# The last projection of a streaming-encoder layer: seven products for eight over pairs of chunks

## The chip, the cores and the metric

The kernel runs on one core of a Trainium2 chip. The metric is device time in microseconds (us) of one execution, lower is better. A core has five engines with a queue of instructions each: TensorE (in the profile PE, with its weight loads as PEld), VectorE (DVE), ScalarE (ACT), GpSimd (POOL) and SyncE (SP), which here issues the DMA transfers. They work side by side and wait for each other through semaphores. SBUF is the working memory with 128 partitions, PSUM takes what TensorE accumulates, and HBM is the large memory outside.

## The reference

One layer on a sequence of 2048 rows with 1024 channels, in float32. Two branches (a causal convolution and stick-breaking attention) are gated and merged to `y`, and a last projection goes back to the residual stream:

```python
mod = c_act @ w_ada[l] + b_ada[l]
shift, scale, gate = jnp.split(mod[:, None, :], 3, axis=-1)
h = rms_norm(x, norm_g[l]) * (1.0 + scale) + shift
u = h @ w_in[l]
...
y_a = conformer_conv_branch(glu_in, gate_a, w_dw[l], b_dw[l], ln_g[l], ln_b[l], w_conv_out[l])
...
o = stick_breaking_attention(q, k, v).reshape(bsz, seq, D_SB)
y_b = (o * jax.nn.silu(gate_b)) @ w_sb_out[l]
y = jax.nn.sigmoid(m_a) * y_a + jax.nn.sigmoid(m_b) * y_b
x = x + gate * (y @ w_out[l])
```

The last line is what is changed: a matrix of 1024 x 1024 times `y`, for 2048 columns.

## The kernel before

Everything lies with channels on the partitions. The 1024 channels are eight rows of 128 (`KC`), the 2048 positions are four chunks of 512 (`CH`, `NCH`). A float32 product is made of three float32r matmuls (`mm3`, line 135): each operand is split into a rounded part, cast by ACT, and a rest, subtracted by DVE (or POOL, for weights in `load_piece`); then hi x hi, hi x lo and lo x hi are added in PSUM.

The kernel has three parts: projections and convolution; attention, with the filling of merge gates between its steps; and the last stage, which this change is about. Its pieces:

- `y_tiles(ch, ...)` (line 1035) makes the gated sum of a chunk. For each of eight rows it multiplies the outputs of the two branches (`za`, `zb`, four tiles each) by the combined weights `w_cs`, 2 x 4 x 3 matmuls into PSUM tiles `p`; DVE multiplies them by the merge gates `ma` and `mb` loaded from HBM, adds them, and the sum is split into `yh` (ACT, line 1061) and `yl` (DVE, line 1062).
- `load_za` and `load_zb` (lines 1012, 1022) load the branch outputs of a chunk through small buffers `io` (four of them, shared with the gates and the tiles of x) and split them by `split_z` (line 1008); for `zb`, POOL first multiplies attention output and gate (line 1030).
- `out_tile(ch, j, ...)` (line 1067) is the last projection for one row of one chunk: 8 x 3 matmuls into a PSUM tile `po`, then one DVE operation (line 1073) that multiplies by `gate` and adds x, and a store.
- The weights `w_out` stay in SBUF: `resident` (line 999) loads and splits them once, during the first chunk; row 0 in pool `wr`, on the left side of SBUF, rows 1 to 7 in pool `wor` on the right. The `w_cs` rows 2 to 7 are in `wr` too. The tiles of `y` and `z` are in pool `yp` on the left.

Chunk 0's gated sums begin while attention ends (from `others`, line 1115): from there on the memory of the normalised input is free, and pools `wr` and `yp` take it. The order afterwards (line 1166): rest of chunk 0's gated sums, loads of chunk 1's `z` tiles, eight `out_tile`s of chunk 0, gated sums of chunk 1, and so on. TensorE's order is written out by hand only through attention (`pin`); in the last stage a scheduler orders each engine's instructions ahead of time, by the order of the code and by what is ready in its own reckoning, and on the chip each engine keeps that order. All transfers of the last stage are issued on the SP queue.

Of the kernel before, what the change touches and what calls it, by code (L numbers as in the profile page):

```python
# [18 lines left out]
P = 128  # L19
# [31 lines left out]
def trunk_kernel(  # L51
# [122 lines left out]
    def hT(g):  # L174
        return hT_[g]

# [695 lines left out]
    with ExitStack() as s2:  # L872
# [124 lines left out]
        wcs, wo = {}, {}  # L997
# [7 lines left out]
        def io(name):  # L1005
            return yp.tile([P, CH], F32, tag="io", name=name, bufs=4)
# [4 lines left out]

        def load_za(ch):
            z = []
            for kc in range(JC):
                t = yp.tile([P, 2, CH], F32R, tag=f"za{kc}", name=f"za{kc}")
# [6 lines left out]
        def load_zb(ch):  # L1022
            z = []
            for kc in range(JC):
                t = yp.tile([P, 2, CH], F32R, tag=f"zb{kc}", name=f"zb{kc}")
# [9 lines left out]
        def y_tiles(ch, za, zb, psum, y):  # L1035

            for j in range(KC):
# [20 lines left out]
                nc.vector.tensor_tensor(out=ma, in0=ma, in1=mb, op=ALU.add)  # L1058
                hi = yp.tile([P, CH], F32R, tag=f"yh{j}", name=f"yh{j}")
                lo = yp.tile([P, CH], F32R, tag=f"yl{j}", name=f"yl{j}")  # L1060
                nc.scalar.copy(out=hi, in_=ma)
                nc.vector.tensor_tensor(out=lo, in0=ma, in1=f(hi), op=ALU.subtract)
                y[0].append(hi)
                y[1].append(lo)
                yield

        def out_tile(ch, j, y, psum):
            ts_ = slice(ch * CH, (ch + 1) * CH)
            xt = io("xt")
            nc.sync.dma_start(xt, x_t[j][:, ts_])  # L1070
            ps = psum("po")
            dense(ps, wo[j], y, KC)
            nc.vector.scalar_tensor_tensor(out=xt, in0=ps, scalar=gate[:, j:j + 1], in1=xt,
                                           op0=ALU.mult, op1=ALU.add)
            nc.sync.dma_start(out_t[j][:, ts_], xt)
# [16 lines left out]
        prev = held = ygen = wr = yp = None  # L1092
        y = ([], [])
# [5 lines left out]
        for n_, u in enumerate(units + [None]):  # L1099
# [15 lines left out]
            def others(q, half):  # L1115

                nonlocal nf, ny, ygen, wr, yp
# [5 lines left out]
                if q == LAST and not half:  # L1123
# [3 lines left out]
                    with tc.high_priority(offset=0):  # L1127
                        za = load_za(0)
                        zb = load_zb(0)
                        wcs[1] = load_piece(wpa, w_cs[1])  # L1130
                    ygen = y_tiles(0, za, zb, lambda n: psum(n), y)
# [34 lines left out]
    with s3:  # L1166
        wor = s3.enter_context(tc.tile_pool(name="wor", reuse_waits="tile", bufs=1, side="right"))
        pd = s3.enter_context(tc.tile_pool(name="pd3", reuse_waits="tile", bufs=2, space=PSUM))
        psum = lambda n: pd.tile([P, CH], F32, tag=n, name=n, bufs=4 if n == "po" else 2)
        for ch in range(NCH):  # L1170
            if ch:
                y = ([], [])
                ygen = y_tiles(ch, za, zb, psum, y)
# [58 lines left out]
```

## Time and profile before

| | |
|---|---|
| median of 3 runs | 1876.35 us (1873.36 to 1876.59) |
| the profiled execution's own time | 1877.81 us |
| its span in the profile | 1876.1 us |
| granted TensorE clock, mean | 0.993 |
| first `po` matmul | at 1560.6 us |

The span is from the first to the last recorded instruction of the profiled execution. A row of grouped instructions names line, engine, operation, the tiles written and read, shapes and count; then busy time and mean duration in ns, then the engine's idle time before them and what ended it. A row in order of time has the start, the duration and what ran. The table's last row is from the view of the tile `po`.

### The profile page before, as it was taken

What the parts mean: (1) busy time and instruction counts of PE and PEld (TensorE: products, weight loads), DVE (VectorE), ACT (ScalarE), POOL (GpSimd) and SP (SyncE); (2) the same over time, 40 slices, a digit from 0 to 9 for tenths busy, and PEclk for the clock granted to TensorE, in tenths of its full rate; (3) what the DMA queues carried; (4) which work ended last, traced back from release to release, by engine and by line L of the source; (5) the groups of instructions that cost most, each with busy time, mean ns of one, the idle gap of its engine ahead of it and who ended that gap; (6) DMA issues with size and microseconds to landing.
All of it is one profiled execution on the core that took longest, in us unless ns stands there. A gap on an engine that the chain in (4) does not pass through costs nothing.

```text
span 1876.1 us, 27226 instructions
## 1 busy us (share of the span) xinstructions
PE 1797.0 (96%) x9612; PEld 1517.0 (81%) x9612; DVE 1228.2 (65%) x1696; ACT 812.8 (43%) x1880; POOL 681.3 (36%) x899
## 2 busy tenths in 40 slices
PE   6899999999999998999999999999999899999999
PEld 5888889899888977778877778777788677888887
DVE  7646578888879354467777777777777895334341
ACT  5465113232231122267766777776777752010110
POOL 0343111111121143466666666666666641010100
PEclk9999999999999999999999999999999999999999
DMA  8553402325132443432232323132322446353532
GB/s 288 169 186 105 137 29 80 90 67 148 45 104 93 157 141 118 149 128 81 79 96 68 102 63 109 61 93 70 99 65 88 131 143 215 107 163 96 164 95 79
DMA packets 117596, 211.08 MB, mean 113 GB/s; under 512 B 15442, under 2 KB 27730, under 8 KB 117460
## 3 DMA queue, kind: packets, MB, share of 16 engines
q1 hardware_dynamic: 116308, 207.24, 35.5%
q10 hardware_dynamic: 1152, 2.10, 0.3%
q8 instruction: 76, 1.25, 0.3%
q14 instruction: 60, 0.49, 0.1%
HBM read 137.98 MB, written 71.30 MB: 112 GB/s over the span
## 4 chain that ended last, share of the span: by engine, by line
PE 72%; DVE 8%; POOL 6%; issue 5%; DMA 5%; ACT 4%; SPq 1%; DVEq 0%; ACTq 0%; POOLq 0%
PE pd L115 38%; PE po L115 9%; PE p L115 8%; PE av L115 5%; PE pT L120 5%; PE z L115 5%; POOL w L952 3%; DVE sc L945 2%; POOL wlo L103 1%; ACT z L941 1%; DMA xt<-in_x_n_dram 1%; PE pt L120 1%; DVE tlo L979 1%; DMA wa<-in_w_ada_dram 1%; DMA gt<-ga 1%
## 5 line engine op out<-in xcount | busy, mean ns | idle before, releaser
L952 POOL TENSOR_TENSOR w<-w,sc 128x512 f32<-128x512 f32 (+1 forms) x320 | 361.6, 1130 | 251.8 <-DVE sc L945 179.1
L115 PE MATMUL pd<-hhi,whi 128*128 128x512 f32 x1024 | 413.4, 404 | 1.0 <-ACT vsg L858 1.0
L115 PE MATMUL pd<-hhi,wlo 128*128 128x512 f32 x1024 | 402.7, 393 | 0.0
L115 PE MATMUL pd<-hlo,whi 128*128 128x512 f32 x1024 | 402.5, 393 | 0.0
L945 DVE TENSOR_TENSOR_SCAN sc<-z,sc,w 128x512 f32<-128x512 f32 x192 | 245.0, 1280 | 90.9 <-ACT z L941 83.6
L103 POOL TENSOR_TENSOR wlo<-wl,whi 128x512 fp32r<-128x512 f32 x88 | 131.3, 1503 | 401.4 <-ACT whi L102 401.2
L115 PEld LDWEIGHTS pd<-hhi,wlo 128*128 128x128 f32 x1024 | 193.5, 189 | 42.5 <-POOL wlo L103 0.2
L940 ACT ACTIVATE w<-z 128x512 f32<-128x512 f32 (+1 forms) x320 | 172.2, 538 | 125.7 <-PE z L115 100.0
L115 PEld LDWEIGHTS pd<-hhi,whi 128*128 128x128 f32 x1024 | 195.5, 191 | 35.4 <-ACT vsg L858 1.4
L115 PEld LDWEIGHTS pd<-hlo,whi 128*128 128x128 f32 x1024 | 194.3, 190 | 34.3
L979 DVE TENSOR_TENSOR tlo<-pT,thi 128x512 fp32r<-128x512 f32 (+1 forms) x320 | 184.2, 598 | 35.8 <-ACT thi L978 32.4
L115 PE MATMUL z<-kt,q 128*128 128x512 f32 (+2 forms) x640 | 192.7, 382 | 5.0 <-DVE sc L945 3.5
L978 ACT CAST thi<-pT 128x512 fp32r<-128x512 f32 (+1 forms) x320 | 165.4, 527 | 61.3 <-PE pT L120 57.4
L120 PE MATMUL pT<-ident,w 128*128 128x128 f32 x1088 | 173.1, 275 | 9.8 <-POOL w L952 9.5
L120 PEld LDWEIGHTS pT<-ident,w 128*128 128x128 f32 x1088 | 137.5, 141 | 45.9 <-POOL w L952 14.5
L115 PE MATMUL pd<-whi,hhi 128*128 128x256 f32 x608 | 169.7, 287 | 3.6 <-ACT hhi L131 1.9
L941 ACT ACTIVATE z<-z 128x512 f32<-128x512 f32 (+1 forms) x320 | 171.7, 537 | 0.0
L115 PE MATMUL pd<-whi,hlo 128*128 128x256 f32 x608 | 167.0, 285 | 2.3 <-DVE hlo L131 1.7
L115 PE MATMUL pd<-wlo,hhi 128*128 128x256 f32 x608 | 154.0, 284 | 0.0
L949 DVE TENSOR_TENSOR_SCAN sc<-z,tri 128x512 f32<-128x512 f32 (+3 forms) x128 | 104.4, 819 | 53.9 <-ACT z L941 41.9
L115 PE MATMUL av<-tlo,vt 128*128 128x512 f32 (+1 forms) x320 | 123.2, 385 | 14.0 <-DVE tlo L979 10.9
L115 PEld LDWEIGHTS z<-kt,q 128*128 128x128 f32 x640 | 109.6, 189 | 24.1 <-DVE sc L945 5.4
(284 smaller groups left out, 3108.4 us busy)
## 6 DMA issues: line engine op xcount, KB each, us to landing
wl<-in_w_in_dram SPq DMA_DIRECT2D x64, 256.0 KB, 2.9
wa<-in_w_ada_dram SPq DMA_DIRECT2D x24, 512.0 KB, 5.1
wl<-in_w_qkv_dram SPq DMA_DIRECT2D x36, 256.0 KB, 2.7
xt<-in_x_n_dram SPq DMA_DIRECT2D x16, 512.0 KB, 5.5
vst<-st SPq DMA_DIRECT2D x64, 128.0 KB, 2.0
kt<-kst SPq DMA_DIRECT2D x32, 256.0 KB, 2.8
vt<-vst SPq DMA_DIRECT2D x32, 256.0 KB, 2.7
q<-qst SPq DMA_DIRECT2D x32, 256.0 KB, 2.8
```

The costliest lines, as they stand in the source:

```text
L103: (lo_eng or nc.gpsimd).tensor_tensor(out=lo[:, s], in0=wl, in1=f(hi[:, s]), op=ALU.subtract)
L115: i = nc.tensor.matmul(*a, **k)
L120: i = nc.tensor.transpose(*a)
L940: nc.scalar.activation(out=w[:, lo:], in_=z[:, lo:], func=AF.Sigmoid, scale=HD ** -0.5)
L941: nc.scalar.activation(out=z[:, lo:], in_=z[:, lo:], func=AF.Sigmoid, scale=-HD ** -0.5)
L945: nc.vector.tensor_tensor_scan(out=s[:, 1:], data0=z, data1=w, initial=s[:, 0:1], op0=ALU.mult, op1=ALU.bypass)
L949: nc.vector.tensor_tensor_scan(out=s[:, lo + 1:], data0=z[:, lo:], data1=tri[:, :CH - lo], initial=1.0, op0=ALU.mult, op1=ALU.max)
L952: nc.gpsimd.tensor_tensor(out=w[:, lo:], in0=w[:, lo:], in1=s[:, lo:CH], op=ALU.mult)
L978: nc.scalar.copy(out=thi[:, :n], in_=pT[:, :n])
L979: nc.vector.tensor_tensor(out=tlo[:, :n], in0=pT[:, :n], in1=f(thi[:, :n]), op=ALU.subtract)
```

## The change

Chunks are taken in pairs. The last projection of a pair is a product of 2 x 2 blocks: the weights are halved by input rows and by output rows (512 x 512 each), `y` by input rows and by chunk. Instead of eight products of such blocks there are seven, of sums or differences of blocks, and each product is added to one or two blocks of the result (12 additions in all). The table `SEVEN` has, for each product, the terms of the weights, the terms of `y`, and the blocks it is added to with their signs; `LASTS` says after which product a block is complete.

- `operands` loads halves of weight rows raw (512 columns, 256 KB each) through `io`, now of eight buffers; where two terms belong to an operand POOL adds or subtracts them (`combined`); then `split_z` casts on ACT and subtracts on DVE. Weights and sums of `y` are `A` and `B`, four tiles each, in two sets with the tags `z` and `o`; these tags are also those of the `za` and `zb` tiles. One set is made while the product before uses the other. All are in `yp`, but the `B` tiles of set `o`, which are in a new pool `yr` on the right.
- `product` has 4 rows x 4 x 3 matmuls into `po`, then per row one or two DVE operations that add the product, times `gate` or its negative `ngate`, to an accumulator `acc` (12 buffers in a pool `ya`, loaded with x at its first use); a complete one is stored.
- The gated sums of a pair are made one after the other and kept unsplit as float32 (`y`); the split of `y` and the resident `w_out` are gone. Chunk 1's `z` tiles are loaded right after attention, chunk 2's during the last product of the first pair, chunk 3's before chunk 2's gated sums.

```diff
+    SEVEN = {
+        2: (((1, 0, 1), (1, 1, 1)), ((0, 0, 1),), ((1, 0, 1), (1, 1, -1))),
+        4: (((1, 1, 1),), ((1, 0, 1), (0, 0, -1)), ((0, 0, 1), (1, 0, 1))),
+        1: (((0, 0, 1), (1, 1, 1)), ((0, 0, 1), (1, 1, 1)), ((0, 0, 1), (1, 1, 1))),
+        6: (((1, 0, 1), (0, 0, -1)), ((0, 0, 1), (0, 1, 1)), ((1, 1, 1),)),
+        3: (((0, 0, 1),), ((0, 1, 1), (1, 1, -1)), ((0, 1, 1), (1, 1, 1))),
+        7: (((0, 1, 1), (1, 1, -1)), ((1, 0, 1), (1, 1, 1)), ((0, 0, 1),)),
+        5: (((0, 0, 1), (0, 1, 1)), ((1, 1, 1),), ((0, 0, -1), (0, 1, 1))),
+    }
+    LASTS = {(1, 0): 4, (1, 1): 3, (0, 0): 5, (0, 1): 5}
+    H = KC // 2
...
-            return yp.tile([P, CH], F32, tag="io", name=name, bufs=4)
+            return yp.tile([P, CH], F32, tag="io", name=name, bufs=8)
...
+        def operand(q, half, i):
+            pool = yr if (q, half) == ("o", "b") else yp
+            return pool.tile([P, 2, CH], F32R, tag=f"{q}{half}{i}", name=f"{q}{half}{i}")
...
-                t = yp.tile([P, 2, CH], F32R, tag=f"za{kc}", name=f"za{kc}")
+                t = operand("zooz"[ch], "a", kc)
...
-                nc.vector.tensor_tensor(out=ma, in0=ma, in1=mb, op=ALU.add)
-                hi = yp.tile([P, CH], F32R, tag=f"yh{j}", name=f"yh{j}")
-                lo = yp.tile([P, CH], F32R, tag=f"yl{j}", name=f"yl{j}")
-                nc.scalar.copy(out=hi, in_=ma)
-                nc.vector.tensor_tensor(out=lo, in0=ma, in1=f(hi), op=ALU.subtract)
-                y[0].append(hi)
-                y[1].append(lo)
+                y[ch, j] = (yr if ch % 2 else yp).tile([P, CH], F32, tag=f"y{j}", name=f"y{j}")
+                nc.vector.tensor_tensor(out=y[ch, j], in0=ma, in1=mb, op=ALU.add)
                 yield
...
+        def combined(terms, part, to):
+            a, b = terms[0], terms[-1]
+            if a is b:
+                return part(a)
+            t = to(a)
+            nc.gpsimd.tensor_tensor(out=t, in0=part(a), in1=part(b),
+                                    op=ALU.add if b[2] > 0 else ALU.subtract)
+            return t
+        turn = [0]
+        def operands(m, ch):
+            q = "zo"[turn[0] % 2]
+            turn[0] += 1
+            A, B = [], []
+            for j in range(H):
+                A.append(operand(q, "a", j))
+                w = {}
+                for t in SEVEN[m][0]:
+                    w[t] = io("w")
+                    nc.sync.dma_start(w[t], w_out[j + H * t[0]][:, t[1] * CH:(t[1] + 1) * CH])
+                split_z(combined(SEVEN[m][0], lambda t: w[t], lambda t: w[t]), A[j])
+                B.append(operand(q, "b", j))
+                split_z(combined(SEVEN[m][1], lambda t: y[ch + t[1], j + H * t[0]],
+                                 lambda t: io("sum")), B[j])
+            return A, B
+        acc = {}
+        def product(m, ch, A, B, psum):
+            for j in range(H):
+                ps = psum("po")
+                for kc in range(H):
+                    s = slice(kc * P, (kc + 1) * P)
+                    mm3(ps, A[j][:, 0, s], A[j][:, 1, s], B[kc][:, 0, :], B[kc][:, 1, :],
+                        kc == 0, kc == H - 1)
+                for r, c_, sign in SEVEN[m][2]:
+                    row, g = j + H * r, ch + c_
+                    ts_ = slice(g * CH, (g + 1) * CH)
+                    if (row, g) not in acc:
+                        acc[row, g] = ya.tile([P, CH], F32, tag="acc", name="acc", bufs=12)
+                        nc.sync.dma_start(acc[row, g], x_t[row][:, ts_])
+                    o = acc[row, g]
+                    nc.vector.scalar_tensor_tensor(
+                        out=o, in0=ps, scalar=(gate if sign > 0 else ngate)[:, row:row + 1],
+                        in1=o, op0=ALU.mult, op1=ALU.add)
+                    if LASTS[r, c_] == m:
+                        nc.sync.dma_start(out_t[row][:, ts_], o)
...
+                    ngate = yp.tile([P, KC], F32, name="ngate")
+                    nc.vector.tensor_scalar(out=ngate, in0=gate, scalar1=-1.0, scalar2=None,
+                                            op0=ALU.mult)
...
-        wor = s3.enter_context(tc.tile_pool(name="wor", reuse_waits="tile", bufs=1, side="right"))
+        yr = s3.enter_context(tc.tile_pool(name="yr", reuse_waits="tile", bufs=1, side="right"))
...
+        za, zb = load_za(1), load_zb(1)
+        steps(ygen)
+        steps(y_tiles(1, za, zb, psum, y))
+        ya = s3.enter_context(tc.tile_pool(name="ya", reuse_waits="tile", bufs=1, side="right"))
+        for ch in (0, 2):
             if ch:
+                za3, zb3 = load_za(3), load_zb(3)
+                steps(y_tiles(2, za, zb, psum, y))
+                steps(y_tiles(3, za3, zb3, psum, y))
+            order = list(SEVEN)
+            nxt = operands(order[0], ch)
+            for i, m in enumerate(order):
+                A, B = nxt
+                if i + 1 < len(order):
+                    nxt = operands(order[i + 1], ch)
+                elif ch == 0:
+                    za, zb = load_za(2), load_zb(2)
+                product(m, ch, A, B, psum)
```

## What was predicted, with its working

> **What bounds the kernel now.** I read the page's busy times first, then the chain of work that ended last, in order of time, then groups by line.
>
> ```profile
> span 1876.1 us, 27226 instructions
> PE 1797.0 (96%) x9612; PEld 1517.0 (81%) x9612; DVE 1228.2 (65%) x1696; ACT 812.8 (43%) x1880; POOL 681.3 (36%) x899
> ```
>
> ```profile
> 1567.41 39.93 PE po L115 x170
> 1607.33 43.52 PE p L115 x192
> 1650.86 44.64 PE po L115 x192
> 1695.50 43.52 PE p L115 x192
> 1739.03 44.64 PE po L115 x192
> 1783.67 43.52 PE p L115 x192
> 1827.19 44.66 PE po L115 x192
> 1871.85 0.02 issue
> 1871.87 0.75 DVE xt L1073
> ```
>
> The second fence has start, length and what worked. From 1567.41 us to the end nothing but TensorE stands in the chain: gated sums (`p`) and last projection (`po`) take turns, and one VectorE operation and a store follow. So this stage is worth its matmuls, and a change there counts in full unless another engine takes over. The other engines have room, as two stretches of 20 us show (columns: busy us of PE, PEld, DVE, ACT, POOL, then granted clock, DMA share, GB/s):
>
> ```profile
> 1700.00:1720.00 20.00, 20.00 (x90) 16.57 (x89) 9.94 (x15) 2.48 (x4) 0.00 (x0) 1.00 0.33 93
> 1840.00:1860.00 20.00, 20.00 (x87) 16.09 (x86) 2.25 (x3) 0.00 (x0) 0.00 (x0) 1.00 0.28 90
> ```
>
> **Matmuls.** Before, `po` has 4 chunks x 8 rows x 8 x 3 = 768 matmuls; at 44.64/192 = 0.2325 us that is 178.6 us. After, 2 pairs x 7 products x 4 x 4 x 3 = 672. `p` runs at 43.52/192 = 0.2267 us. Why `po` is slower is seen by weight row:
>
> ```profile
> L115 PE MATMUL po<-yh,wo0h x32: 389/389/505, 1560.6 to 1831.8; 128*128 128x512 f32 x32
> L115 PE MATMUL po<-yh,wo2h x32: 395/396/396, 1573.6 to 1843.0; 128*128 128x512 f32 x32
> ```
>
> (ns: shortest, median, longest.) `wo0` lies in pool `wr` on the left, `wo1` to `wo7` in `wor` on the right; the moving operand is the same. The new weights `A` all lie in `yp`, on the left, so I take 0.2267: 152.3 us. Half the products read `B` from `yr` on the right, against weights on the left; no row has that pairing. Bounds are 0.2267 and 0.2325; I take the middle for those 336, +1.0. Term: 153.3 - 178.6 = **-25.3 us** (-26.3 to -22.4).
>
> **The hand-over to the stage.** TensorE waits once:
>
> ```profile
> 1566.60 0.51 PE L115 MATMUL po<-yh,wo0h 128*128 128x512 f32 x1 [1.06 <-ACT yh L1061]
> 1567.41 0.50 PE L115 MATMUL po<-yl,wo0h 128*128 128x512 f32 x1 [0.30 <-DVE yl L1062]
> ```
>
> That is 1.36 us for the last split of `y`. After, chunk 1's gated sums follow directly and need no split of `y`; late next are chunk 1's `z` tiles, whose 12 loads take the queue places of the 16 loads of `w_out`. I take **-1** (-1.4 to 0). All 32 splits of `y` go; none was waited for otherwise.
>
> **What each product adds.** Rows for the prices (count, then busy us and mean ns):
>
> ```profile
> L1073 DVE SCALAR_TENSOR_TENSOR xt<-po,gate,xt 128x512 f32<-128x512 f32 x32 | 23.7, 750 | 100.2 <-PE po L115 92.0 <-DMA xt<-in_x_t_dram 8.2
> L1010 DVE TENSOR_TENSOR za<-n,za 128x512 fp32r<-128x512 f32 x8 | 5.5, 690 | 4.2 <-ACT za L1009 4.0
> L1010 DVE TENSOR_TENSOR zb<-o,zb 128x512 fp32r<-128x512 f32 x8 | 9.0, 1124 | 14.7 <-ACT zb L1009 14.4
> L1009 ACT CAST za<-n 128x512 fp32r<-128x512 f32 x8 | 5.0, 620 | 7.4 <-PE p L115 3.9 <-DMA n<-za 3.5
> L1030 POOL TENSOR_TENSOR o<-o,gb 128x512 f32<-128x512 f32 x8 | 10.3, 1294 | 163.3 <-DMA gb<-gb 87.2 <-DMA o<-o 76.1
> ```
>
> Per pair of chunks: 7 x 8 = 56 splits (a cast at 0.62 on ACT, a subtraction at 0.69 on DVE), 12 x 4 = 48 accumulations at 0.75 on DVE, and, counting the two-term entries of the table, 40 sums at 1.29 on POOL. Alone, ACT has 34.7 us, POOL 51.6, DVE 38.6 + 36.0 = 74.6, beside TensorE's 76.7 (153.3/2). Each engine fits, DVE barely. But they don't run side by side. The `zb` split costs 1124 ns where the same operation on `za` costs 690; in order of time:
>
> ```profile
> 1747.59 1.29 POOL L1030 TENSOR_TENSOR o<-o,gb 128x512 f32<-128x512 f32 x1 [0.59 <-DMA gb<-gb]
> 1747.68 1.74 DVE L1010 TENSOR_TENSOR zb<-o,zb 128x512 fp32r<-128x512 f32 x1 [3.01 <-ACT zb L1009]
> 1665.85 1.30 POOL L1030 TENSOR_TENSOR o<-o,gb 128x512 f32<-128x512 f32 x1 [0.35 <-DMA gb<-gb]
> 1666.19 1.51 DVE L1010 TENSOR_TENSOR zb<-o,zb 128x512 fp32r<-128x512 f32 x1 [4.05 <-ACT zb L1009]
> 1489.36 1.73 POOL L952 TENSOR_TENSOR w<-w,sc 128x512 f32<-128x512 f32 x1
> 1489.88 1.27 DVE L979 TENSOR_TENSOR tlo<-pT,thi 128x512 fp32r<-128x512 f32 x2
> ```
>
> A split begun inside a POOL sum ends 0.54 us after it (1749.42 against 1748.88; 1667.70 against 1667.15): it waits, then runs. `tlo`, with an input from PSUM, does not (two in 1.27 us inside a POOL operation). So accumulations, which read PSUM, can lie beneath sums; splits can't. Sum and split take 1.29 + 0.54 = 1.83 us.
>
> Take the six products during which products 2 to 7 are prepared (the first is prepared beside the gated sums): 36 sums, 48 splits, 40 accumulations, beside 6 x 10.95 = 65.7 us of TensorE. If every sum holds up one split and all accumulations lie beneath sums: 36 x 1.83 + 12 x 0.69 = 74.2. Operands are double-buffered, one product ahead; of a product's 10.95 us eight splits take 5.5, so 5.4 of lateness is covered. Not hidden: 74.2 - 65.7 - 5.4 = 3.1. If no accumulation lies beneath: another 30.0, 33.1 in all. If sums meet no splits (48 x 0.69 + 30 = 63.1): 0. Where sums pace splits, as in the `zb` rows, DVE is free between them, so I stay near 3.1; but at each of six boundaries four tiles of `B` come free at once, their splits burst, and the last row's accumulations (ten in all) queue behind. Half of those in the open: 3.8. Per pair **6.9**, both **+13.8** (0 to +66).
>
> In the in-order queues: behind a waiting split stand accumulations, and TensorE waits for these only when four `po` buffers are full; on SP, loads for the next product stand ahead of the x loads and stores, and `io` has 8 buffers.
>
> **Rest.** Chunk 2's `z` tiles are now loaded during product 7 of the first pair (10.95 us), not during 44.64 us of `po`: eight splits and eight accumulations are 11.5 us of DVE, and TensorE needs the last four only after 12 matmuls, 2.7 us. I take +1 (0 to +4). At the end two accumulations follow the last matmul for one: 0.75, and the last store waits behind up to seven others: **+1** (0.75 to +3).
>
> Sum: -25.3 - 1 + 13.8 + 2 = **-10.5 us**. From the profiled execution's own 1877.8 (span 1876.1 and 1.7 around it) that is 1867.3; it lies 1.5 above the median of the runs, 1876.35, so I forecast **1866**.
>
> **Where the skill differs.** The Trainium skill, GPSIMD Engine Reference, section Elementwise — side-by-side cycle accounting, gives a POOL operation on two tensors about 2.6 cycles an element; 512 elements at the 1.2 GHz used there are 1.11 us, an estimate from that page. By it sums and splits would need 36 x (1.11 + 0.54) + 8.3 = 67.7 us, 5.4 is covered, and the whole would be about -23. The trace has 1.29, and I go by it.
>
> **Rivals.** *Clean gain* (0.18): sums run while DVE accumulates or idles, as POOL does work ahead into `io` buffers; then 0 for the 13.8: -24.3, so 1852; 1849 with the lower bounds of the other terms, and up to 1858 with a little loss. For it: DVE alone fits. Against it: 82 us of sums and splits (40 x 1.29 + 56 x 0.54) on 76.7.
>
> *Slower* (0.30): in-order DVE leaves accumulations in the open. Gain and loss balance when the loss per pair is 12.1 (25.3 + 1 - 2, halved), 9.0 above the 3.1, that is 12 of 40 accumulations. With half of them: 3.1 + 15 = 18.1 per pair, -24.3 + 36.2 = +12: 1888. For it: 74.6 us on DVE has no slack, and each burst of splits meets POOL's work for the product after.
>
> *Transfers* (0.10): weights are loaded 96 times instead of 16, 256 KB each. During four products of seven 8 of them are due for the next, and 4 of x or stores beside them: 12 x 0.262 = 3.15 MB in 10.95 us, 287 GB/s.
>
> ```profile
> 1555.00:1560.00 5.00, 5.00 (x24) 4.14 (x23) 4.12 (x7) 1.47 (x4) 0.00 (x0) 1.00 0.75 215
> 1585.00:1590.00 5.00, 5.00 (x23) 4.04 (x22) 2.07 (x3) 0.00 (x0) 0.00 (x0) 1.00 0.82 288
> ```
>
> At 288 they just fit (10.9 us); at 215 they take 14.6, 3.7 too many, less the 5.4: 9.4 per pair. In place of the 6.9 (both wait at once) that gives 1871. The Trainium skill, DMA: Bandwidth & Descriptors, Specifications, names 358 GB/s per core, by which this rival would fall away; no row reaches it.
>
> **How the numbers follow.** The forecast, gain partly given back (1858 to 1872), has 0.42. A measurement here tells about 0.2%, 3.8 us, so *same* is 1872.6 to 1880.1. Faster: 0.38 of the forecast, 0.18 clean, 0.05 of transfers, 0.61. Same: 0.04, 0.05 of transfers, 0.03 of slower, 0.12. Slower: 0.27. Range **1850 to 1892**: nearly the clean gain's lower end, and a little more than half the accumulations in the open; the forecast's own is 1858 to 1872.
>
> **What would show it.** Matmuls of `po` 672, 0.2267 apart; sums about 1.3 us; splits near 1.1 where they meet sums, 0.69 elsewhere; accumulations 0.75; idle TensorE before products 3 to 7 put down to a split on DVE, 7 us per pair; GB/s below 290. I am wrong if the idle time is put down to loads of `w`, lies in the gated sums, or if DVE is full through the products and accumulations hold `po` buffers.

## The result, and the profile after

| | before | after |
|---|---|---|
| median | 1875.16 us | 1898.47 us (1896.43 to 1900.18, 4 executions) |
| ratio, 95% interval | | 1.0124 (1.0107 to 1.0142) |
| profiled execution's own time | 1877.81 us | 1897.0 us |
| its span | 1876.1 us | 1895.3 us |
| first `po` matmul | 1560.6 us | 1605.5 us |

The change is slower by 1.2%. Forecast were 1866 and a range of 1850 to 1892: a gain was forecast, and the time is a loss and lies above the range. First the busy times of the changed kernel's page:

```profile
span 1895.3 us, 27512 instructions
...
PE 1785.4 (94%) x9516; PEld 1505.1 (79%) x9516; DVE 1345.6 (71%) x1825; ACT 846.6 (45%) x1944; POOL 796.8 (42%) x979
```

TensorE has 96 instructions less, the 768 - 672 matmuls. DVE and POOL have 117.4 and 115.5 us more. Before, the chain of work that ended last held only `po` and `p` behind 1567 us. A part of the same chain after, in order of time (start, length, what):

```profile
1610.68 2.57 DMA w<-in_w_out_dram
1614.96 1.67 POOL sum L1090
...
1623.73 1.75 POOL w L1090
1627.96 1.32 DVE acc L1129 x2
1630.10 1.70 DVE za L1027
...
1642.09 4.69 DMA w<-in_w_out_dram
...
1856.77 33.62 PE po L115 x144
```

TensorE is gone from this chain for the first products of each pair; loads of weights, sums on POOL, splits and accumulations on DVE follow one another. Where the time lies is seen by stages. The rows are the seven products of the first pair, the gated sums of chunks 2 and 3, the products of the second pair, then 20 us of the first and 17 of the second (length, busy us of PE, PEld, DVE, ACT, POOL, granted clock, DMA share, GB/s):

```profile
1605.46:1702.50 97.04, 83.98 (x338) 66.81 (x337) 86.33 (x104) 34.16 (x60) 57.62 (x41) 0.93 0.62 196
1702.50:1797.50 95.00, 90.65 (x385) 73.55 (x384) 44.70 (x66) 7.35 (x12) 9.94 (x8) 0.96 0.52 175
1797.50:1890.40 92.90, 80.31 (x337) 63.90 (x335) 81.09 (x98) 27.67 (x49) 54.16 (x37) 0.96 0.50 163
1620.00:1640.00 20.00, 16.59 (x55) 13.07 (x56) 18.97 (x24) 5.81 (x10) 16.97 (x12) 0.77 0.46 147
1703.00:1720.00 17.00, 12.65 (x51) 9.88 (x50) 10.55 (x17) 3.00 (x5) 5.43 (x4) 0.88 0.96 340
```

336 matmuls at the 0.2267 us of the forecast are 76.2 us, and the products take 97.0 and 92.9. Two things are to be read from the first row: TensorE is busy 83.98 of 97.04, so it idles 13.1 us; and its 84.0 are 7.8 more than 76.2 at a granted clock of 0.93. The fourth row shows where: 0.77 around 1630. For the idle time, TensorE's waits from 1605 to 1891 us (us in total, times, longest):

```profile
PE po L115 <- DVE acc L1129: 25.6, 10, 5.2
PE p L115 <- DVE ma L1078: 4.3, 1, 4.3
```

No product waits for an operand or a load: each wait is for an accumulation (line 1129), that is, for a PSUM buffer `po` to come free. Why the accumulations were late stands in VectorE's instructions in order of time, while the first product runs (start, length, what; in brackets the idle time before it and what ended it):

```profile
1609.36 0.69 DVE L1027 TENSOR_TENSOR za<-w,za 128x512 fp32r<-128x512 f32 x1 [3.73 <-ACT za L1026]
1609.97 0.68 DVE L1027 TENSOR_TENSOR oa<-w,oa 128x512 fp32r<-128x512 f32 x1
1610.57 1.79 DVE L1027 TENSOR_TENSOR ob<-sum,ob 128x512 fp32r<-128x512 f32 x1
...
1612.89 1.39 DVE L1027 TENSOR_TENSOR oa<-w,oa 128x512 fp32r<-128x512 f32 x1
...
1614.81 0.68 DVE L1027 TENSOR_TENSOR ob<-sum,ob 128x512 fp32r<-128x512 f32 x1
1615.41 1.77 DVE L1027 TENSOR_TENSOR oa<-w,oa 128x512 fp32r<-128x512 f32 x1
...
1618.31 1.75 DVE L1027 TENSOR_TENSOR ob<-sum,ob 128x512 fp32r<-128x512 f32 x1
1619.97 0.74 DVE L1129 SCALAR_TENSOR_TENSOR acc<-po,gate,acc 128x512 f32<-128x512 f32 x1
```

The first row of products starts at 1605.46 and has 12 matmuls, 2.7 us; its accumulation runs at 1619.97, some 11.8 us after its data. Until then the in-order queue stands 3.73 us for the cast of the first product's own last weight tile (`za`), splits it, and works on the second product's operands (`oa`, `ob`); four of their eight splits take 1.39 to 1.79 us, the others 0.68. Four `po` buffers hold one product's four rows, so TensorE ran its 48 matmuls, stood still at 1616.5, and went on at 1621.52. The delay is not made up: DVE is busy 86.33 of the 97.04 us. Of the first pair's operations (mean ns, then the idle time before them and who ended it):

```profile
L1090 POOL TENSOR_TENSOR sum<-y,y 128x512 f32<-128x512 f32 x20 | 29.4, 1474 | 17.1 <-DVE zb L1027 6.4 <-DVE y L1081 3.2 <-DVE ob L1027 2.5
L1090 POOL TENSOR_TENSOR w<-w 128x512 f32<-128x512 f32 x17 | 24.4, 1440 | 7.2 <-DMA w<-in_w_out_dram 5.9 <-DVE za L1027 0.6 <-DVE ob L1027 0.6
L1027 DVE TENSOR_TENSOR ob<-sum,ob 128x512 fp32r<-128x512 f32 x12 | 14.7, 1234 | 1.0 <-ACT ob L1026 1.0
```

Sums take 1.44 to 1.47 us for the 1.29 that I had priced (a sum, too, is held up by a split that came first), and the splits of summed operands about 1.2.

### The profile page after: what moved, and what is told of

Its sections match the earlier page's. It is cut to its first block, busy times and chain, and to the rows that moved or that the text cites. A ratio compares the mean times of both kernels' runs of the same rounds, so it can differ in the third digit from the quotient of the medians.

```text
span 1895.3 us, 27512 instructions
## 1 busy us (share of the span) xinstructions
PE 1785.4 (94%) x9516; PEld 1505.1 (79%) x9516; DVE 1345.6 (71%) x1825; ACT 846.6 (45%) x1944; POOL 796.8 (42%) x979
## 4 chain that ended last, share of the span: by engine, by line
PE 64%; DVE 11%; POOL 8%; DMA 7%; issue 5%; ACT 3%; SPq 1%; DVEq 0%; POOLq 0%; ACTq 0%
PE pd L115 40%; PE p L115 6%; PE av L115 5%; PE pT L120 5%; PE z L115 5%; POOL w L969 3%; DVE sc L962 2%; PE po L115 2%; DMA w<-in_w_out_dram 2%; POOL w L1090 1%; DMA gb<-gb 1%; POOL sum L1090 1%; DVE tlo L996 1%; DVE acc L1129 1%; ACT z L958 1%
## 5 line engine op out<-in xcount | busy, mean ns | idle before, releaser
L120 PEld LDWEIGHTS pT<-ident,w 128*128 128x128 f32 x1088 | 136.9, 140 | 45.2 <-POOL w L969 14.1
```

The source lines that it names most:

```text
L120: i = nc.tensor.transpose(*a)
```

## The experiments

The table gives each stretch from the first start of its matmuls to the first of the next (the last to its end), worked out from one profiled execution of each version, and the time beside the kernel before in the same comparison, both in us. The times of e1 to e4 and e6 to e9 are single executions, the others medians of 4 to 10; e2 and e9 leave out work and don't compute the layer. The kernel before has no pairs of chunks: its four stretches of `po`, less the 1.4 us of waiting, are put as two halves.

| run | what differs from the changed kernel | products 1 | gated sums | products 2 | time | before |
|---|---|---|---|---|---|---|
| before | | 89.6 | 87.04 | 89.6 | 1875.16 | |
| after | | 97.02 | 95.07 | 92.83 | 1898.47 | 1875.16 |
| e1_psum_copy | splits don't meet sums | 88.52 | 103.51 | 85.57 | 1892.61 | 1872.46 |
| e2_no_sums | no sums | 76.40 | 94.64 | 76.55 | 1863.69 | 1872.46 |
| e3_eight_banks | one ring of eight PSUM buffers | 89.56 | 93.54 | 90.05 | 1891.34 | 1872.46 |
| e4_acc_first | accumulations ahead of splits | 96.58 | 95.06 | 93.52 | 1898.51 | 1872.46 |
| e5_weights_ready | weights summed and split ahead | 76.40 | 89.12 | 76.55 | 1933.95 | 1872.76 |
| e6_weight_sums_ready | weights summed ahead | 76.40 | 94.77 | 76.55 | 1894.93 | 1872.76 |
| e7_ready_eight | e5 and eight buffers | 76.40 | 88.37 | 76.55 | 1937.63 | 1872.76 |
| e8_copy_six | e1 and a ring of six | 85.92 | 89.55 | 85.85 | 1873.97 | 1872.76 |
| e9_one_half | one load for each summed weight | 90.46 | 93.95 | 85.25 | 1880.63 | 1875.31 |
| e10_sums_early_eight | weights summed in the first projections, eight buffers | 76.40 | 88.37 | 76.55 | 1873.96 | 1875.31 |
| e12_sums_kept | e8; second pair loads the first pair's sums | 96.12 | 91.10 | 76.55 | 1877.97 | 1874.24 |
| e13_kept_order | e12, another order of products | 90.72 | 95.20 | 76.55 | 1876.10 | 1874.24 |
| e14_kept_by_act | e12, stores issued by ACT | 95.10 | 96.27 | 76.55 | 1880.34 | 1874.54 |
| e15_kept_by_act_order | both | 91.06 | 96.65 | 76.55 | 1876.55 | 1874.54 |
| e16_early_in_turn | e10, sums in program order | 76.40 | 88.37 | 76.55 | 1867.42 | 1873.96 |
| e17_early_pool_queue | e16, pieces' transfers from POOL's queue | 76.40 | 88.37 | 76.55 | 1916.97 | 1873.96 |
| e18_early_act_queue | e16, pieces' transfers from ACT's queue | 76.40 | 88.37 | 76.55 | 1884.58 | 1873.96 |

One more, e11, e10 with four `po` buffers, ran at a granted clock of 0.557 from end to end and can't be compared. The start of attention differs by up to 5.8 us (799.2 to 805.0) between profiled executions with equal code before it, so stretches are compared rather than single times where less than that matters. How far a stretch with waits differs between executions of one version is not known; those without any repeat at 76.40 and 76.55.

The scheduler orders each version anew. From 20 us ahead of the first product on, only e3 keeps VectorE's order of the changed kernel operation for operation; the other versions differ from it by that order too. The order of e2, e6, e9 and e10 is nearly one and the same.

### No sums: what all of it costs

```diff
-            t = to(a)
-            nc.gpsimd.tensor_tensor(out=t, in0=part(a), in1=part(b),
-                                    op=ALU.add if b[2] > 0 else ALU.subtract)
-            return t
+            return part(a)
```

> The 80 sums on POOL are left out (the first term alone is used, the output is not the reference's); every load stays, as do splits and accumulations. Theories 1 and 2: splits at 0.69, DVE has 74.6 us per pair, each stretch of seven products 76 to 80 us, time 1853 to 1864. Theory 3 (transfers): no change, 1890 or more. If plain DVE work bounds it (theory 4): stretches stay above 85 us, 1875 or more.

Measured 1863.69 us. The three stretches, in the columns as above:

```profile
1609.30:1685.86 76.56, 76.56 (x338) 63.22 (x337) 65.63 (x103) 34.14 (x58) 5.63 (x4) 1.00 0.73 239
1685.70:1780.50 94.80, 91.12 (x386) 73.88 (x385) 46.65 (x68) 9.45 (x16) 5.37 (x4) 0.96 0.56 186
1780.34:1856.89 76.55, 76.55 (x337) 62.89 (x335) 61.83 (x97) 27.46 (x46) 0.00 (x0) 1.00 0.56 185
```

TensorE is busy from end to end of both sets of products, at full clock, with all 96 loads still there and moving 239 GB/s. So the matmuls were priced rightly, moving these bytes costs nothing here (the second half of a summed weight is loaded, but nothing reads it or waits for it), and all of the products' loss, 97.02 + 92.83 - 76.40 - 76.55 = 36.9 us, hangs on the sums and on what has to wait for them. The gated sums' 94.64 do not.

### No collisions, more PSUM buffers, another order

`e1_psum_copy` lets ACT copy the rounded half to PSUM, and the split's subtraction reads it there, so it has one input from SBUF; the two buffers come from `p`, which has one of each kind left. `e3_eight_banks` has one ring of eight buffers for all PSUM tiles, `e4_acc_first` has the accumulations scheduled earlier, `e8_copy_six` joins the copy with a ring of six.

```diff
+        def split_w(o, t):
+            nc.scalar.copy(out=t[:, 0, :], in_=o)
+            hp_ = psum("hi")
+            nc.scalar.copy(out=hp_, in_=f(t[:, 0, :]))
+            nc.vector.tensor_tensor(out=t[:, 1, :], in0=o, in1=hp_, op=ALU.subtract)
...
-        psum = lambda n: pd.tile([P, CH], F32, tag=n, name=n, bufs=4 if n == "po" else 2)
+        psum = lambda n: pd.tile([P, CH], F32, tag=n, name=n, bufs={"po": 4, "hi": 2}.get(n, 1))
```

> ACT copies each rounded part once more, into PSUM, and DVE subtracts that copy, so that the split has one SBUF input; sums, splits and their number stay, four po buffers too. Theory 1 (POOL sum and DVE split exclude each other): splits fall from about 1.1 us to 0.7, POOL sums from 1.45 to 1.3, the two stretches of seven products shrink from 97 and 93 us to 78 to 84, time 1866 to 1878. Theory 2 (the place of the accumulations in DVE's queue, behind splits that wait for their sums): the sums still come one by one, the lag at the head of each pair stays, 1885 to 1893. Theory 3 (transfers): within 4 us of 1898.

Measured 1892.61. In the first pair, with the same columns as after:

```profile
L1090 POOL TENSOR_TENSOR sum<-y,y 128x512 f32<-128x512 f32 x19 | 24.8, 1312 | 8.7 <-DVE za L1100 6.5 <-DVE oa L1100 1.3 <-DVE ob L1100 0.6
L1100 DVE TENSOR_TENSOR ob<-sum,hi 128x512 fp32r<-128x512 f32 x12 | 8.2, 682 | 4.2 <-ACT hi L1099 4.0
```

The splits fall from 1234 to 682 ns, the sums to 1312: the collision is real and goes with the second SBUF input. The Trainium skill, SBUF — State Buffer, section Who interferes with whom, says that a DVE instruction with at most one SBUF input, outside its two-port modes, does not contend with GpSimd; these rows agree. Without it the products are 8.5 and 7.3 us shorter, less than half the loss; and one `p` buffer of a kind costs the gated sums 8.4 (one wait of 12.3 us). What the products wait for now is the operands:

```profile
PE p L115 <- DVE ma L1078: 12.3, 1, 12.3
PE po L115 <- DVE zb L1100: 5.9, 5, 1.9
PE po L115 <- DVE ob L1100: 4.2, 4, 2.0
```

The next two leave the splits as they are:

```diff
-        psum = lambda n: pd.tile([P, CH], F32, tag=n, name=n, bufs=4 if n == "po" else 2)
+        psum = lambda n: pd.tile([P, CH], F32, tag="ps", name=n, bufs=8)
```

> All eight PSUM banks are one ring of buffers, so that eight po tiles may wait for DVE instead of four; DVE's order is the same. Theory 2: TensorE no longer waits for accumulations in the first three products, 10 to 16 us per pair come back, 1868 to 1880. Theory 1 or 4 (DVE is full, whatever the buffers): the wait moves to operands or to the next gated sums, 1890 to 1898.

```diff
-                    nc.vector.scalar_tensor_tensor(
+                    with tc.high_priority(offset=400):
+                        nc.vector.scalar_tensor_tensor(
...
```

> Accumulations get a higher priority, so that they come earlier in DVE's order, in front of splits of the next product. Theory 2: the lag at the head of each pair shrinks by 4 to 8 us, 1880 to 1890. Theory 1: the same work collides in the same way, 1894 to 1900.

TensorE's waits in the products, with eight buffers:

```profile
PE po L115 <- DVE zb L1027: 8.6, 9, 2.4
PE po L115 <- DVE ob L1027: 8.3, 8, 2.4
```

and with the accumulations ahead:

```profile
PE po L115 <- DVE acc L1130: 15.6, 14, 3.4
PE po L115 <- DVE ob L1027: 4.8, 3, 2.8
PE po L115 <- DVE zb L1027: 4.8, 3, 2.7
```

Eight buffers win 7.5 and 2.8 us, though VectorE's order is the same; then the operands are what is late. Accumulations moved ahead win nothing (190.1 us of products for 189.9): what they gain, the splits behind them lose. This other order on VectorE only changed which of the two TensorE waits for.

```diff
-                split_z(combined(SEVEN[m][0], lambda t: w[t], lambda t: w[t]), A[j])
+                split_w(combined(SEVEN[m][0], lambda t: w[t], lambda t: w[t]), A[j])
...
+        psum = lambda n: pd.tile([P, CH], F32, tag="hi" if n == "hi" else "ps", name=n, bufs=2 if n == "hi" else 6)
```

> e1 (splits that don't collide with sums) with six banks in one ring for po and p, and two for the copies. Theory A: the late first sums of each pair remain, stretches 84 to 88 us, 1886 to 1892. Theory B the same; if the four po buffers were what is left after e1, 78 to 81 us, 1875 to 1882.

1873.97 beside 1872.76, each stretch within the first theory's 84 to 88 us, the time below what both expected: 18.1 us of products come back and 5.5 of the gated sums, and the loss against before is gone, but no gain is left. What is late now stands further up, in the waits during the first pair's products:

```profile
POOL w L1090 <- DMA w<-in_w_out_dram: 13.6, 10, 2.7
```

### Fewer loads, fewer sums

`e9_one_half` loads one half for each summed weight, and POOL adds it to itself: as many sums and splits, 28 loads a pair instead of 48.

```diff
-                for t in SEVEN[m][0]:
-                    w[t] = io("w")
-                    nc.sync.dma_start(w[t], w_out[j + H * t[0]][:, t[1] * CH:(t[1] + 1) * CH])
-                split_z(combined(SEVEN[m][0], lambda t: w[t], lambda t: w[t]), A[j])
+                w = io("w")
+                t = SEVEN[m][0][0]
+                nc.sync.dma_start(w, w_out[j + H * t[0]][:, t[1] * CH:(t[1] + 1) * CH])
+                split_z(combined(SEVEN[m][0], lambda t: w, lambda t: w), A[j])
```

> Where a weight operand has two terms, one half is loaded and POOL adds it to itself (the output is not the reference's): 40 sums, 56 splits, 48 accumulations per pair as in the changed kernel, but 28 loads and 28 io buffers for weights where it has 48. Theory A (work of POOL and DVE): the stretches of seven products stay at 88 to 97 us. Theory B (loads of halves through eight io buffers, which make the sums late): they fall to 76 to 82 us.

1880.63: 6.6 and 7.6 us of products come back, with collisions and four buffers still there; 90.46 is within the first theory's range, 85.25 in neither. One thing the loads do is seen at the head of the first pair. In the changed kernel and here the first weight load is issued 15 us ahead of the first product; that product's last weight tile is split 3.9 us into it there, with eight halves to load, and 3.1 us ahead of it here, with four loads for the same four sums. How much of the 14.1 us are the loads alone is not shown, as VectorE's order changed with them; e2 shows that their bytes cost nothing by themselves.

`e6_weight_sums_ready` makes the 20 sums of weights once, between the merge gates, and stores them in HBM; each pair then loads 28 ready halves and has 20 sums, of `y` only. Its core:

```diff
+                        nc.gpsimd.tensor_tensor(out=w[0], in0=w[0], in1=w[1],
+                                                op=ALU.add if terms[1][2] > 0 else ALU.subtract)
+                        nc.sync.dma_start(wA_d[m, j], w[0])
...
+                w, terms = io("w"), SEVEN[m][0]
+                nc.sync.dma_start(w, wA_d[m, j] if len(terms) > 1 else w_out[
+                    j + H * terms[0][0]][:, terms[0][1] * CH:(terms[0][1] + 1) * CH])
+                split_z(w, A[j])
```

> Only the sums of weights are made ahead and stored; each product loads one raw tile per row, splits it as before, and still adds y on POOL. Theory A: 56 splits and 48 accumulations are 74.6 us on DVE, 20 sums hold up some splits by 0.5 to 1.1 us each: stretches 80 to 88 us, 1870 to 1882. Theory B (what starved the sums was the ring of eight io buffers and the loads of halves, not DVE): with one buffer per weight tile the stretches fall to 76 to 79 us, as with everything ready, 1862 to 1869.

```profile
1640.56:1717.12 76.56, 76.56 (x338) 63.23 (x337) 69.69 (x100) 32.57 (x55) 31.96 (x21) 1.00 0.59 183
```

That is the first pair; the second is the same. The products run without a gap, although every split still has two SBUF inputs, 20 sums a pair still meet them and `po` has four buffers. With half of the sums and fewer loads, the collisions and the PSUM buffers cost nothing that is seen. But the time is 1894.93: attention's first scores matmul starts at 834.1, where it was 800.2 in the changed kernel. `e5_weights_ready`, with the weights' splits ahead too,

> The weight operands of all seven products are summed, split and stored once, during the merge gates ahead of attention, and each product loads its four tiles ready made, in both pairs; sums and splits of y stay. Theory A (the wait comes from DVE and POOL together: splits and accumulations in one queue, sums that exclude splits): DVE has 28 splits and 48 accumulations per pair, 55 us, and the 20 sums left fit beside; stretches of seven products 76 to 79 us, time 1860 to 1868. Rival: the work ahead of attention costs there what it saves here, 1870 to 1885.

starts attention at 880.4 and takes 1933.95, ratio 1.032 (1.0288 to 1.0351), more than its rival said; `e7_ready_eight`, the same with the ring of eight, takes 1937.63.

> e5 with all eight PSUM banks in one ring. Theory A: nothing waits for po buffers any more, so no change of the stretches, within 3 us of e5. If accumulations still stand behind splits of y: 2 to 6 us less than e5.

### Keeping the first pair's sums

`e12_sums_kept` takes e8, stores each weight sum when the first pair has made it, and loads it in the second. `e13` takes the products in the order 2, 6, 4, 1, 3, 7, 5. `e14` and `e15` issue the stores from ACT's queue behind the cast.

```diff
+                if ch and len(terms) > 1:
+                    s_ = io("w")
+                    nc.sync.dma_start(s_, wS_d[m, j])
+                else:
...
+                    if len(terms) > 1:
+                        nc.sync.dma_start(wS_d[m, j], s_)
```

> e8, and the 20 sums of weights made for the first pair are stored and loaded in the second, where POOL has 20 sums instead of 40 and 28 loads of weights instead of 48. Theory A and B agree that the second stretch falls from 86 to 77 us; the first stays at 86 or gets 1 to 3 us longer for its 20 more stores; time 1862 to 1868, faster than both kernels by the second stretch alone.

> e12 with the products in the order 2, 6, 4, 1, 3, 7, 5, so that no two products of eight sums follow each other. If what is left of the first stretch after e8 (10 us) is POOL's eight sums twice in a row, it falls from 86 to 78 to 82 us, time 1856 to 1863. If it is the loads of halves through eight io buffers, which a product of eight sums needs whatever its place, the first stretch stays within 2 us of e12.

> e12 with the stores of the kept sums issued by ACT behind the split's casts, not by SP among the loads. If the stores waiting for their sums held up the loads behind them on SP's queue, the first stretch falls from 96 to 86 to 88 us as in e8, the second stays at 77, time 1862 to 1868. If the 20 stores cost by their bytes, the first stretch stays above 92 us, 1872 or more.

> e14 in the order 2, 6, 4, 1, 3, 7, 5. If products of eight sums in a row matter, the first stretch is 80 to 84 us, time 1857 to 1863; if the loads through the io buffers do, it is within 2 us of e14.

The second pair's products run at 76.55 in all four, and the rest gives the gain back: the first pair's take 90.72 to 96.12 against e8's 85.92, and in three of them the gated sums are longer by 5.6 to 7.1. Another order of the products (e13, e15) takes 5.4 and 4.0 us off the first pair, between what its two expectations said. Ratios to before: 1.0022 (1.0012 to 1.0031), 1.0011 (1.0001 to 1.002), 1.0038 (1.0026 to 1.0051), 1.0012 (1.0003 to 1.0022). The waits of the queue that issues the transfers point to the stores: in e12 the queue's longest wait in total from 1504 to 1701 us is at the store (line 1119), which waits for the sum with the next weights' loads behind it.

```profile
SPq L1119 <- POOL w L1090: 44.8, 19, 4.3
```

With the stores on ACT's queue that wait is gone, but a buffer is free for its next load only when its store has landed:

```profile
SPq L1116 <- DMA wS<-w: 10.4, 3, 6.0
```

A store holds one of the same eight buffers that the loads wait for, and with it the loads behind on SP's queue; that these 10.4 us are the whole of the difference is not shown.

### Summing early, spread out

`e10_sums_early_eight` makes the weights' sums during the first projections, in pieces of 256 columns with buffers of their own, at low priority, and has the ring of eight.

```diff
+            def weight_sum(m, j, q):
+                w = []
+                for i, t in enumerate(SEVEN[m][0]):
+                    w.append(cvp.tile([P, 256], F32, tag=f"pw{i}", name=f"pw{i}", bufs=1))
+                    c0 = t[1] * CH + q * 256
+                    nc.sync.dma_start(w[i], w_out[j + H * t[0]][:, c0:c0 + 256])
+                nc.gpsimd.tensor_tensor(out=w[0], in0=w[0], in1=w[1],
+                                        op=ALU.add if SEVEN[m][0][1][2] > 0 else ALU.subtract)
+                nc.sync.dma_start(wA_d[m, j][:, q * 256:(q + 1) * 256], w[0])
...
```

> As e6, the 20 sums of weights once and ahead, but during the first projections, in pieces of 256 columns with buffers of their own, so that no weight load of those stages waits for them; and eight PSUM banks in one ring. Both stretches 76 to 78 us as in e6, the gated sums of chunks 2 and 3 near 90; with attention beginning when it did before (802 to 806 us), 1853 to 1860, faster than both kernels. Rival: the early sums cost as in e6, attention begins 30 us late, 1885 or more.

```profile
1628.71:1705.27 76.56, 76.56 (x338) 63.23 (x337) 71.65 (x103) 32.22 (x54) 32.06 (x20) 1.00 0.63 187
1705.11:1793.64 88.53, 88.53 (x386) 72.19 (x385) 46.67 (x68) 11.00 (x19) 10.98 (x8) 1.00 0.56 184
```

Those are the first pair and the gated sums. TensorE does not wait once in the last stage, and the stage is 44 us shorter than the changed kernel's. Attention starts at 823.8, and the time is 1873.96 against 1875.31: ratio 1.000 (0.9986 to 1.0013). The last three runs move the pieces about: in program order at every second step (e16), and then from the queues of POOL (e17) and ACT (e18).

```diff
             if nticks[0] % 2 == 0 and sums:
-                with tc.high_priority(offset=-LATE):
-                    sums.pop(0)()
+                sums.pop(0)()
```

> The weights' 20 sums are made once, in 256-column pieces, during the first projections, as in the run with early sums and eight PSUM banks (1873.96 us; products at 76.56 and 76.55 us, attention's first scores matmul 20 us later than before's 803.1), but each piece stands in program order at every second step of the projections, and is not deferred to low priority. Theory (the 20 us come of the pieces' load, sum and store standing in clumps on SP's queue ahead of the projections' own loads and stores): spread out they cost at most 7 us, attention begins by 810, the products stay at 76.5, and the time is 1854 to 1862 us, faster than both kernels. Rival (the projections have no room for 40 loads, sums and stores wherever they are put): attention begins at 820 or later again and the time is 1870 to 1878.

> The same pieces in the same places, their loads and stores issued from POOL's queue in place of SP's. Theory (SP's queue is what the projections wait for): attention begins by 806 and the time is 1850 to 1858 us. Rival (it is not the queue but POOL's own work, which now waits for each piece's load of some 3 us with the projections' other work of POOL behind it): attention begins at 815 to 830 and the time is 1866 to 1880.

> The same pieces, their loads and stores issued from ACT's queue. Theory of SP's queue: attention begins by 806, 1850 to 1858 us. Rival (each issue and each store's wait for its sum holds ACT's evictions and casts of the projections): attention begins at 815 or later, 1866 us or more.

`e16` takes 1867.42 us (1861.59 to 1879.72, six executions) beside 1873.96: ratio 0.996 (0.9943 to 0.9976). It is the one version that beats both kernels, by 0.4%. Its profiled execution is the slowest of the six, and there attention starts at 824.4, as in e10 and not by the theory's 810; what the other five do in the projections no profile shows. In this profile, the stretch 250 to 450 us, its one long wait of TensorE, and the two longest waits of SP's queue in it:

```profile
250.00:450.00 200.00, 182.09 (x1136) 164.71 (x1135) 156.82 (x190) 46.41 (x231) 61.10 (x47) 0.95 0.39 120
```

```profile
PE pt L120 <- DVE qn L321: 17.9, 1, 17.9
```

```profile
SPq L724 <- POOL pw L722: 73.3, 24, 4.5
SPq L721 <- DMA wA<-pw: 24.0, 23, 2.5
```

In the same stretch of before TensorE is busy for all 200 us. SP's queue stands 97 us for the pieces, each store waiting for its sum and each load for the store before it, and the projections' own transfers stand behind. TensorE's long wait can be followed back to that. The tile `qlo` has one buffer; its content was made by 309.8 us, but SP issues its store only at 333.53, with four stores and nine loads of the pieces in between, and VectorE waits for that store's landing. The third line is the same store in before, where `qlo` was made by 310.41:

```profile
337.32 0.69 DVE L341 TENSOR_TENSOR qlo<-pt,qhi 128x512 fp32r<-128x512 f32 x1 [21.16 <-DMA qst<-qlo]
333.53 0.54 SPq L346 DMA_DIRECT2D qst<-qlo  x1
310.44 0.45 SPq L323 DMA_DIRECT2D qst<-qlo  x1
```

From POOL's queue (e17) it is worse: 1916.97, ratio 1.023 (1.0207 to 1.0253), attention at 861.5, with POOL 99.84 us busy in that stretch for 61.10. TensorE's two longest waits from 22 to 450 us are again for `qn` and for the rests of weights that POOL makes:

```profile
PE pt L120 <- DVE qn L321: 29.0, 2, 27.2
PE pd L115 <- POOL wlo L103: 22.2, 5, 11.7
```

From ACT's (e18) it is 1884.58, ratio 1.0054 (1.0039 to 1.0069), attention at 831.1. So in e16's profile it is SP's queue that holds the projections, but the theory that another queue would be free of this falls: the pieces cost more on each of the two. The rivals hold in their direction, and POOL's price was beyond its rival's range.

## Why the prediction was wrong

Its terms beside what the two profiled executions differ by, 1897.0 - 1877.8 = 19.2 us (the medians differ by 23.3):

| step | predicted | measured | from |
|---|---|---|---|
| matmuls | -25.3 | -25.6 | 76.40 + 76.55 for 178.6 |
| hand-over | -1 | 0 | start of `po` 44.8 us later than before, for 43.5 of gated sums and 1.4 of wait |
| products | +13.8 | +36.9 | 20.6 and 16.3 above the matmuls |
| chunk 2's tiles | +1 | +8.0 | 95.07 for 2 x 43.52 |
| end | +1 | +0.6 | 4.9 us from last matmul to end, for 4.3 |

The measured terms add up to 19.9. The 0.7 too many lie in before's `po`: its four stretches hold 180.7 us, where price and wait give 180.0. Attention's last matmul ends at 1540.4 in both. At the hand-over the wait of 1.4 us is gone as forecast, but chunk 1's gated sums take 1.3 us more than before's: their matmuls, which read the tiles of set `o`, stand 234 ns apart, those with set `z` 227.

**Right:** the matmul term, with `B` from the right side too; the counts; the collision of sums and splits (1.2 us in the mean for a summed operand's split, 1.39 to 1.79 in the long ones shown above), though it lengthens the sums too, to 1.44 and 1.47; and that the bytes are hidden (e2). The prediction's own sign of being wrong came as it was put: DVE nearly full through the products (86.33 of 97.04 us), and accumulations that hold `po` buffers.

**The step that failed** is the sum under *What each product adds*: 36 sums at 1.83 us and 12 splits, less 65.7 us of TensorE, less "of a product's 10.95 us eight splits take 5.5, so 5.4 of lateness is covered". With the bursts it gave 6.9 us per pair, and 20.6 and 16.3 were measured. What failed in it is the cover of 5.4 us and the place of the accumulations, which it had beneath the sums, all but half of ten. The runs show four reasons.

First, the cover was not there. Double-buffered operands cover a late operand. But VectorE's queue is in order, and what a late split delays is also the accumulation behind it, whose four `po` buffers are one product deep. The prediction named that and priced it at nothing beyond 3.8 us; in the profile all 25.6 us that TensorE waits in the products are for it. With eight buffers a part of the cover appears, 10.2 us (e3); with the accumulations moved ahead the wait is in part for operands, and no shorter (e4).

Second, the first product's preparation was put at nothing ("the first is prepared beside the gated sums"). In after its last weight tile is split 3.9 us into it, and the second product's splits stand behind that one, ahead of the first accumulation.

Third, a sum was priced as if its inputs were there. It waits for loads, and these for one of eight buffers: with 28 loads a pair for 48, e9 wins 14.1 us, in part perhaps by its other order on VectorE, and without the 20 sums of weights e6 wins the other 22.8. That the chain load, sum, cast, split, buffer free again is longer than its busiest engine is my reading; no run measures its length.

Fourth, TensorE loses twice by idling: the 13.1 us of waits in the first pair come with 7.4 us (83.98 - 76.56) of longer busy time, in the second 12.6 with 3.8. Of these, 6.3 and 2.3 us are matmuls at half the granted clock: TensorE is busy 12.5 and 4.6 us in stretches where it is 0.50.

The parts overlap: collisions 15.8 us of the products (e1), PSUM buffers 10.2 (e3), loads 14.1 (e9), collisions and PSUM buffers together 18.1 (e8), and half of the sums with their loads all 36.9 (e6). I read them as links of one chain: taking away one moves the wait to the next, as the waits of e1, e3 and e8 show. Which link was the tightest can't be said in one number.

Of the **rivals**, *slower* had the mechanism, accumulations in the open on an in-order VectorE, at 1888 and 0.30. Its term for the products, 2 x 18.1 = 36.2, all but meets the measured 36.9, with some luck: it had no half clock, and it subtracted the cover of 5.4 us that was not there. Its time, 12 us above before's, is short of the profiled 19.2 by chunk 2's tiles, 8.0 for 1. *Clean gain* is refuted by after. *Transfers* as bandwidth is refuted by e2; as a wait for buffers it is a part, but not as it was put.

**Chunk 2's tiles**, +1 predicted, cost 8.0: the second row of the stages has 4.35 us idle and a clock of 0.96. In its first 17 us the DMA share is 0.96, and TensorE's one wait there, 4.3 us, is for `ma`. The chain that ended last runs there through the last `z` tiles, a gate and TensorE:

```profile
1705.61 1.54 POOL o L1052
1708.54 3.85 DMA o<-o
1713.68 3.77 DMA ma<-ma
1718.18 63.21 PE p L115 x264
```

I had counted only VectorE's work for these tiles, not the transfers that stand in one queue with the gates. With eight buffers and fewer loads the stretch is 88.37 without a wait (e10), so 6.7 of the 8.0 are the wait and its half clock, and 1.3 are in the spacing of chunk 2's matmuls, which read set `o` (234 ns apart; chunk 3's, with set `z`, 227).

**Open:** where e16 wins its time, and how much of the projections' loss (some 20 us in the profiled execution) could be had back by stores that don't hold the queue.

## What to carry to other kernels

When work moves to another engine, add up the chain a piece of it must go through (buffer, load, sum, cast, split) and what stands behind it in each in-order queue, not only each engine's total; a cover counts only if it lies between the late instruction and the one that waits. A trick that saves TensorE an eighth of a product is paid in operand sums: make those that don't change once and in an earlier stage, and look at that stage's queues as closely as at the one that gains. An experiment that removes one link and sees the wait move to the next has found one link of a chain; remove the whole chain first (e2) to know what there is to win.

## What was not expected of the hardware

- TensorE's granted clock is 0.50 for stretches of 3.41 or 6.83 us after some waits: the trace has matmuls 427 ns apart there, 227 otherwise. The Trainium skill, TensorE: Matmul & The Clock Gate, section What's actually happening, tells of a gate with a window of 3413 ns; the lengths agree with one and two such windows. The same section of the Trainium skill names an idle window of about 3.4 us as what throttles the clock. Here the trace differs: in the changed kernel's last stage the clock fell after waits of 1.89, 2.15, 4.35, 4.98 and 5.21 us, and did not after six of 0.70 to 3.39 us, so the length of the wait alone does not decide. The waits in the products cost 57 and 30% more than their length: 13.1 + 7.4 and 12.6 + 3.8 us in the two pairs.
- Matmuls of `po` with `B` on the right side of SBUF and `A` on the left run at the same 227 ns as those with both on the left; before, with the weights on the right, `po` took 232. The side of the weights does not decide alone, as the prediction had it: the gated sums that stream the tiles `oa`, which lie on the left, past weights on the left, stand 234 ns apart (e10, after). What decides is open.
- 340 GB/s were moved over 17 us; in before's rows quoted above the most was 288.
